# A two-layer hybrid decoder on eight cores: another QKV chain, element-wise work offered to more engines, second norms in a fixed order, and weight loads moved in their queue

## The chip, the cores and the metric

One Trainium2 chip, eight cores, the same program on each with other data: core c takes prompt sequence c and four of the 32 decode rows. The metric is the device time of the slowest core in microseconds. Some runs fall into a slower state, in which one die's cores show a lower granted clock (in one run of the first batch below, four cores took 1698 to 1702 us at 0.81 and the other four 1444 to 1450 at 0.99).

## The reference, cut to what matters

```python
# per layer, for prompt rows (causal) and decode rows (with caches)
h = rmsnorm(x, norm1_g);  proj = h @ w_in               # u | q k v | gb gc gh
y_pool = pool_mix(u)                                    # windows 2/4/8/16
q = partial_rope(rmsnorm(q, q_norm_g), pos)             # per head of 64; rotary on the first 16 dims
k = partial_rope(rmsnorm(k, k_norm_g), pos)             # k and v also go out as the new caches
y_attn = three dilated windows of 2 heads, merged by their softmax denominators
y_conv = gb * conv3(gc * gh)
x = x + concat(y_pool, y_attn, y_conv) @ w_out
x = x + square(relu(rmsnorm(x, norm2_g) @ w_up)) @ w_down
# two layers; 2048 prompt rows + 32 decode rows per core = 5 blocks of 416 columns
```

## The kernel before

The kernel plans its own instruction streams when it is built. Each piece of work is a small process with a priority. It asks for operations with an estimated cost, waits for events and takes buffers from pools. A list scheduler steps through estimated time and appends each operation to one engine's program. `anyof` offers an operation to several engines, and the one that can take it first in the plan gets it. **The plan is static: on the chip every engine runs its list in order, and a PE instruction that waits holds up all behind it.** Weights are loaded by DMAs that the Pool engine issues, in the order of Pool's list.

```python
def dp(n, fn, r, w):                       # DVE or Pool
    return anyof(dve2(n, fn, r, w), pool(n, fn, r, w))

def sumsq(l, which, b, X, s, s, src):      # sum of squares of block b (second norm, and layer 1's first)
    yield acq(PNORM)
    ...
    yield ops(act(BL, ... AF.Square ...))                       # chunk 0 into acc
    for c in range(1, 8):
        ...
        yield ops(act(BL, ... AF.Square ...))                   # ACT
        K.spawn(freeing(dp(BL, ... acc = acc + t ...)))         # DVE or Pool
    bi = yield late(1, lambda bi: pe([... matmul(ones, acc) ...]))

def qkv(l, blk, g, pr):                    # one tile: 256 rows, q k v of two heads; PQKV = Pool([0] * 2) in flight
    ...
    pb0 = yield late(J, ... 16 matmuls into two PSUM banks ...)
    yield ops(act(256 * J, ... Square of q,k from PSUM into sqv ...))
    ...                                    # v * row scale, from PSUM on DVE
    yield ops(dve(256 * J, ... tensor_reduce sqv -> ss ...))
    yield ops(act ... Ln ..., act ... Ln ...);  yield ops(act ... Exp ...)          # rs
    yield ops(dve(256 * J, ... q4 = PSUM q,k * rs ...))         # only now can the two banks go
    yield wait(ev("vq", l, blk, g, pr));  K.release(BANKS, ...);  K.release(PQKV, 0)
    ...                                    # rotary on q4, DVE or Pool
    yield ops(anyof(pool(... cast q4 -> qb bf16 ...), dvec(...), act(...)))
    ...                                    # transposes of qb on PE

def up(l, fb, b, fc):
    ...                                    # 8 matmuls, then PSUM * norm scale on DVE
    yield ops(act(BL, ... Relu ...))
    yield ops(act(BL, ... Square -> bf16 ...))

# weights of the first MLP quarter (fb == 0)
wu, wd = proj_done, qk_done + [ev("xres", l, b, 7) for b in (0, 1)]
```

The MLP goes over four quarters of d_ff. A w_up or w_down quarter comes in four pieces of 512 KB (as bf16), and each down-matmul group reads all four pieces of its w_down quarter.

Of the kernel before, what the change touches and what calls it, by code (L numbers as in the profile page):

```python
# [25 lines left out]
BL = NTOK // NB  # L26
# [523 lines left out]
def build_program():  # L550
# [234 lines left out]
    SQ = [m([128, 512], F32, ("sq", i)) for i in range(2)]  # L785
    m = Mem(XO + SV * XB, XO + SV * XB + XB)
# [66 lines left out]

    def pe(items):

        cost, rw = 0.0, []
        for n, _, r, w in items:
            rw.append((cost, r, w))
            cost += max(n / 2400.0 + 0.0025, 0.056)
        return ("pe", cost, lambda: [S.op("pe", fn, r, w) for _, fn, r, w in items], rw)  # L860
# [21 lines left out]
    PQKV = Pool([0] * 2)  # L882
# [95 lines left out]
    def sumsq(l, which, b, X, s, si, src):  # L978
# [24 lines left out]
        else:  # L1003
            ai = yield acq(PSQR)
            acc, ka = sqr(ai), ("sqr", ai)
            yield ops(act(BL, lambda e: e.activation(out=acc, in_=X[:, si, 0, :], func=AF.Square), [("x", s, 0)], [ka]))
            for c in range(1, 8):
# [4 lines left out]
                yield ops(act(BL, lambda e: e.activation(out=out, in_=X[:, si, c, :], func=AF.Square), [("x", s, c)], [k]))  # L1012
# [91 lines left out]
    def norm2(l, b):  # L1104
        s = SLOTR[b]
        bi = yield from sumsq(l, 1, b, X, s, s, [ev("xm", l, b, c) for c in range(8)])
        yield wait(*[ev("om", l, x, oc) for x in ((0, 1), (2, 3), (4,), (4,), ())[b] for oc in range(8)], *r_free(l, b))
# [198 lines left out]
    def qkv(l, blk, g, pr):  # L1306
# [52 lines left out]
        yield ops(act(256 * J, lambda e: e.activation(out=sqv, in_=pq[0:R, :, 0:256], func=AF.Square), kp, [ksq]))  # L1359
        rt = RT[0:R, 0, tt:tt + J].unsqueeze(2)  # L1360
        if need:
# [3 lines left out]
            K.spawn(seq([], later(dve(128 * J, lambda e: e.tensor_tensor(out=qv, in0=pq[0:R, :, 256:384], in1=rv_, op=ALU.mult), kp + kt, [kq]), ev("vq", l, blk, g, pr)),  # L1365
                        later(act(128 * J, lambda e: e.copy(out=vd, in_=qs), [kq], kv), ev("vc", l, blk, g, pr))), 1000 * l + 100 + 30 * (blk or 0) + 2 * g + pr + 0.5)
# [4 lines left out]
        o = [dve(256 * J, lambda e: e.tensor_reduce(out=ss[0:R, 0:4 * J], in_=sqv.rearrange("p j (a c) -> p (j a) c", a=4), axis=AX.X, op=ALU.add), [ksq], [kss])]  # L1371
        yield ops(*o)
# [3 lines left out]
        q4 = qf[0:R, 0:J, 0:256].rearrange("p j (a c) -> p j a c", a=4)  # L1376
        rb = rs[0:R, 0:4 * J].rearrange("p (j a) -> p j a", j=J).unsqueeze(3).to_broadcast([R, J, 4, 64])
        yield ops(dve(256 * J, lambda e: e.tensor_tensor(out=q4, in0=pq[0:R, :, 0:256].rearrange("p j (a c) -> p j a c", a=4), in1=rb, op=ALU.mult), kp + [krs], [kq]))  # L1378
        K.release(PS4, s4)
        yield wait(ev("vq", l, blk, g, pr))  # L1380
        for j in range(J):
            K.release(BANKS, pb0 + j)
        K.release(PQKV, 0)
        if g > 0 and not smp:
            K.spawn(vshuffle(l, blk, g, pr, vi), 1000 * l + 100 + 50 * blk)
        ri = yield acq(PROT)
        kr = ("rot", ri)
        t0 = 16 if smp else 4 * blk + tis[0]
        rot = [ROTB[ri][0:R, k, 0:4 * J, :].rearrange("p (j a) c -> p j a c", j=J) for k in range(2)]
        xr = q4[:, :, :, 0:16]  # L1390
        tb = [ROPE[0:R, k, t0:t0 + J, :].unsqueeze(2).to_broadcast([R, J, 4, 16]) for k in range(2)]
        g16 = GQK[0:R, 0:64].rearrange("p (a c) -> p a c", a=4).unsqueeze(1).to_broadcast([R, J, 4, 16])
        yield ops(dp(64 * J, lambda e: e.tensor_tensor(out=xr, in0=xr, in1=g16, op=ALU.mult), [kq, "gqk"], [kq]))  # L1393
        yield ops(*[dp(65 * J, lambda e, k=k: e.tensor_tensor(out=rot[k], in0=xr, in1=tb[k], op=ALU.mult), [kq, "rope"], [kr]) for k in range(2)])  # L1394
        yield ops(*[dp(32 * J, lambda e, h=h, op=op: e.tensor_tensor(out=xr[:, :, :, 8 * h:8 * h + 8], in0=rot[0][:, :, :, 8 * h:8 * h + 8], in1=rot[1][:, :, :, 8 - 8 * h:16 - 8 * h], op=op), [kr], [kq]) for h, op in ((0, ALU.subtract), (1, ALU.add))])
        K.release(PROT, ri)
# [7 lines left out]
        def store():  # L1404
            o = []
            for jj, j in enumerate(tis):
                if smp:
                    for n in range(4):
                        o.append(ld(lambda e, n=n: e.dma_start(out=o_kv_s[g][l, n, WINS[g] - 8:WINS[g], :], in_=qf[8 * n:8 * n + 8, 0, 128:384]), 8192, 1024, r=[kq], slot=("kvo", fi)))
                    continue  # L1410
# [3 lines left out]
                o.append(ld(lambda e, jj=jj, dst=dst: e.dma_start(out=dst, in_=qf[:, jj, 128:384]), 131072, 1024, r=[kq], slot=("kvo", fi)))  # L1414
# [6 lines left out]
        if turn:  # L1421
# [4 lines left out]
        qi, qo = qf[0:R, 0:J, 0:256], qb[0:R, 0:J, :]  # L1426
        yield ops(anyof(pool(256 * J, lambda e: e.tensor_copy(out=qo, in_=qi), [kq], [kb], False), dvec(256 * J, lambda e: e.tensor_copy(out=qo, in_=qi), [kq], [kb]),
                        act(256 * J, lambda e: e.copy(out=qo, in_=qi), [kq], [kb])))
        if need:
# [447 lines left out]
    K.run()  # L1877
    assert K.live == 0

    S.emit(es)  # L1880
    es.close()
    return nc

# [77 lines left out]
```

## Time and profile before

| | before |
|---|---|
| time, median of the first 4 runs (range) | 1462.38 us (1460.24 to 1463.35) |
| spans of the cores in the profile | 1452.6 to 1461.6 us |
| mean granted PE clock | 0.981 to 0.988 |
| PE busy | 1393.2 us, 95% |

In the trace a matmul of the MLP lasts 0.34 us while the next one starts 0.18 us after it, and a matmul at half clock counts as busy all the same, so busy time hides small losses. The lines that concern us carry these numbers in the kernel before: L1702 up-projection, L1724 down-projection, L1333 QKV, L1153 the other projections, L1679 out-projection, L1016 the ones-matmul of a norm's sum, L1716 squared relu, L1378 the q,k product that frees the banks.

### The profile page before, as it was taken

How to read it: one execution, taken by the hardware profiler on the slowest of the kernel's cores; microseconds unless marked ns; L12 is line 12 of the kernel's file. 1: busy time of each engine (PE TensorE's matmuls, PEld its weight loads, DVE VectorE, ACT ScalarE, POOL GpSimd, SP SyncE). 2: the span in 40 equal slices, each digit the busy share in tenths (PEclk: the TensorE clock that was granted, in tenths of full speed). 3: DMA queues.
4: the chain of work that ended last, by engine and by line, in shares of the span. 5: the costliest groups of instructions: out<-in, count | busy, mean ns of one | idle time of the engine just before them, and what ended most of it. 6: DMA issues, size and time to landing. Idle time of an engine off the chain costs nothing.

```text
span 1461.6 us, 28003 instructions; the slowest of 8 cores (1452.6 to 1461.6 us)
## 1 busy us (share of the span) xinstructions
PE 1393.2 (95%) x8921; PEld 793.2 (54%) x8921; DVE 800.9 (55%) x1503; ACT 727.4 (50%) x1536; POOL 323.3 (22%) x495
## 2 busy tenths in 40 slices
PE   6999989899999999999999899996999999999998
PEld 3555656455555555555555565553555555555554
DVE  2878767664444444446577877865344444444443
ACT  4656557674244243347756556567243433523532
POOL 4557546410000000000025654640001001000000
PEclk9999989999999999999999999998899999999999
DMA  9750573880690573152245152489019319200122
GB/s 209 188 81 27 89 141 117 209 117 1 97 170 2 87 104 76 31 93 94 61 91 121 28 99 64 151 169 155 3 34 157 77 17 160 63 28 1 48 94 94
DMA packets 81677, 133.31 MB, mean 91 GB/s; under 512 B 14008, under 2 KB 70520, under 8 KB 81152
## 3 DMA queue, kind: packets, MB, share of 16 engines
q0 software_dynamic: 53952, 79.29, 30.6%
q1 hardware_dynamic: 18880, 49.10, 12.8%
q10 hardware_dynamic: 8704, 3.15, 0.9%
q8 instruction: 75, 1.23, 0.3%
q14 instruction: 66, 0.54, 0.1%
HBM read 159.63 MB, written 47.90 MB: 142 GB/s over the span
## 4 chain that ended last, share of the span: by engine, by line
PE 84%; DMA 5%; issue 3%; DVE 3%; ACT 2%; POOL 2%; DVEq 0%; SPq 0%; ACTq 0%; POOLq 0%
PE psum L1724 31%; PE psum L1702 29%; PE psum L1153 8%; PE psum L1333 7%; PE psum L1679 5%; DMA big<-w_down 3%; DMA big<-xin 2%; PE psum L1548 1%; POOL big L851 1%; PE psum L1439 1%; PE psum L991 0%; DMA big<-xpark 0%; DVE big L1371 0%; PE psum L1523 0%; DVE big L1378 0%
## 5 line engine op out<-in xcount | busy, mean ns | idle before, releaser
L1724 PE MATMUL psum<-big 128*128 128x416 bf16 x2560 | 460.2, 341 | 14.7 <-DMA big<-w_down 10.7
L1702 PE MATMUL psum<-big 128*128 128x416 bf16 x2560 | 457.2, 339 | 2.9 <-DMA big<-w_up 1.3
L1715 ACT ACTIVATE big<-big 128x416 f32<-128x416 f32 x320 | 175.0, 548 | 414.1 <-DVE big L1713 413.2
L1724 PEld LDWEIGHTS psum<-big 128*128 128x128 bf16 x2560 | 250.1, 98 | 217.9 <-issue 21.2
L1702 PEld LDWEIGHTS psum<-big 128*128 128x128 bf16 x2560 | 249.1, 98 | 203.4 <-issue 5.7
L1727 DVE TENSOR_TENSOR big<-psum,big 128x416 f32<-128x416 f32 x320 | 189.1, 591 | 248.0 <-PE psum L1724 248.0
L1713 DVE TENSOR_TENSOR big<-psum,big 128x416 f32<-128x416 f32 x320 | 189.0, 591 | 243.9 <-PE psum L1702 181.8
L1716 ACT ACTIVATE big<-big 128x416 bf16<-128x416 f32 x320 | 174.8, 548 | 41.7 <-PE psum L1702 1.3
L1153 PE MATMUL psum<-big 128*128 128x416 bf16 x880 | 172.0, 346 | 8.7 <-DVE big L1654 2.2
L1333 PE MATMUL psum<-big 128*128 128x384 bf16 (+1 forms) x816 | 144.0, 331 | 4.7 <-ACT big L1535 1.8
L1153 PEld LDWEIGHTS psum<-big 128*128 128x128 bf16 x880 | 84.0, 100 | 76.9 <-issue 18.3
L852 ACT ACTIVATE big<-big 128x416 bf16<-128x416 f32 (+3 forms) x135 | 85.2, 636 | 72.7 <-DVE big L1683 26.8
L1333 PEld LDWEIGHTS psum<-big 128*128 128x128 bf16 (+1 forms) x816 | 78.3, 99 | 58.5 <-issue 10.9
L963 POOL DMA_DIRECT2D big<-w_up x32 | 24.0, 768 | 385.8 <-PE psum L1702 368.2
L1679 PE MATMUL psum<-big 128*128 128x416 bf16 x480 | 88.3, 343 | 1.7 <-DVE big L1378 0.8
L851 POOL TENSOR_SCALAR big<-big 128x416 bf16<-128x416 f32 (+4 forms) x46 | 64.1, 1394 | 51.2 <-DVE big L1683 23.5
L1679 PEld LDWEIGHTS psum<-big 128*128 128x128 bf16 x480 | 46.6, 99 | 40.2 <-issue 4.9
L1683 DVE TENSOR_TENSOR big<-psum,big 128x416 f32<-128x416 f32 x80 | 46.4, 587 | 23.3 <-PE psum L1679 19.5
L1359 ACT ACTIVATE big<-psum 128x512 f32<-128x512 f32 (+1 forms) x54 | 30.7, 569 | 53.8 <-PE psum L1333 52.8
L1394 POOL TENSOR_TENSOR big<-big 128x128 f32<-128x128 f32 (+1 forms) x79 | 41.3, 523 | 61.1 <-DVE big L1393 51.6
L1371 DVE TENSOR_REDUCE big<-big 128x8 f32<-128x512 f32 (+1 forms) x54 | 35.2, 651 | 18.0 <-ACT big L1359 16.1
L1374 ACT ACTIVATE big<-big 128x4 f32<-128x4 f32 (+1 forms) x102 | 30.3, 297 | 27.1 <-DVE big L1371 22.7
(133 smaller groups left out, 1089.7 us busy)
## 6 DMA issues: line engine op xcount, KB each, us to landing
big<-w_up POOLq DMA_DIRECT2D x32, 512.0 KB, 19.0
big<-w_down POOLq DMA_DIRECT2D x32, 512.0 KB, 15.6
kv_s<-c SPq DMA_DIRECT2D x8, 2040.0 KB, 16.9
big<-xin_r POOLq DMA_DIRECT2D x10, 832.0 KB, 13.5
xpark<-big SPq DMA_DIRECT2D x10, 832.0 KB, 4.2
big<-xpark POOLq DMA_DIRECT2D x10, 832.0 KB, 8.8
yout<-big SPq DMA_DIRECT2D x20, 416.0 KB, 2.5
big<-xin POOLq DMA_DIRECT2D x8, 832.0 KB, 13.1
```

The source lines that it names most:

```text
L851: f = lambda e: e.tensor_scalar(out=out, in0=in_, scalar1=g, scalar2=None, op0=ALU.mult)
L852: return anyof(act(n, lambda e: e.activation(out=out, in_=in_, func=AF.Copy, scale=g), r, w, True), dvec(n, f, r, w), pool(n, f, r, w, False))
L1153: bi = yield late(1, lambda bi: pe([(BL, lambda e, d=d: e.matmul(bank(bi)[:, 0:BL], lhsT=wa(l, nm, i, d), rhs=HT[:, d, BL * b:BL * b + BL] ...
L1333: pb0 = yield late(J, lambda pb0: pe([(384, lambda e, d=d, j=j, jj=jj: e.matmul(bank(pb0 + jj)[0:R, 0:384].rearrange("p (k n) -> p k n", k ...
L1679: bi = yield late(1, lambda bi: pe([(BL, lambda e, c=c: e.matmul(bank(bi)[:, 0:BL], lhsT=WO[c // 2][:, c % 2, 128 * oc:128 * oc + 128], rh ...
L1683: yield ops(dve(BL, lambda e: e.tensor_tensor(out=X[:, s, oc, :], in0=bank(bi)[:, 0:BL], in1=X[:, s, oc, :], op=ALU.add), [("ps", bi), ("x ...
L1702: bi = yield late(1, lambda bi: pe([(BL, lambda e, d=d: e.matmul(bank(bi)[:, 0:BL], lhsT=WU[i][:, d, 128 * fc:128 * fc + 128], rhs=HT[:, d ...
L1713: yield ops(dve(BL, lambda e: e.tensor_tensor(out=rl, in0=bank(bi)[:, 0:BL], in1=VB[b], op=ALU.mult), [("ps", bi), kvb(b)], [kr]))
L1715: yield ops(act(BL, lambda e: e.activation(out=rl, in_=rl, func=AF.Relu), [kr], [kr]))
L1716: yield ops(act(BL, lambda e: e.activation(out=AT[a][:, fc, :], in_=rl, func=AF.Square), [kr], [("at", a, fc)]))
L1724: bi = yield late(1, lambda bi: pe([(BL, lambda e, f=f: e.matmul(bank(bi)[:, 0:BL], lhsT=WD[i][:, f, 128 * oc:128 * oc + 128], rhs=AT[a][: ...
L1727: yield ops(dve(BL, lambda e: e.tensor_tensor(out=X[:, s, oc, :], in0=bank(bi)[:, 0:BL], in1=X[:, s, oc, :], op=ALU.add), [("ps", bi), ("x ...
```

## The change

Its intent: free the QKV banks early, run rotary beside the norm instead of after it, take load off ACT, finish norms in the order in which the MLP wants them, and have each first w_down quarter land right behind its w_up quarter.

```diff
+    def squared(n, out, x, r, w):
+        f = lambda e: e.tensor_tensor(out=out, in0=x, in1=x, op=ALU.mult)
+        return anyof(act(n, ... AF.Square ...), dve2(n, f, r, w), pool(n, f, r, w))
-    PQKV = Pool([0] * 2)
+    PQKV = Pool([0] * 3)
 # sumsq
-            yield ops(act(BL, ... AF.Square ...))
+            yield ops(squared(BL, ...))                          # both places
 # norm2(l, b)
+        i = ORDER[l][0].index(b)
+        if i:
+            yield wait(ev("n2", l, ORDER[l][0][i - 1]))
         bi = yield from sumsq(l, 1, b, X, s, s, ...)
+        K.fire(ev("n2", l, b))
 # qkv
+        K.spawn(... anyof(dve(256 * J, qf = PSUM q,k), act(...)) ...)      # copy out at once
+        def free_banks():
+            yield wait(ev("vq", ...), ev("qe", ...), ev("sqd", ...))       # v, copy, square done
+            ... K.release(BANKS, ...); K.release(PQKV, 0) ...
+        def rope():
+            yield wait(ev("qe", ...))                                      # on the unscaled copy
+            ... rotary as before ...
         yield ops(act(... Square ...)); reduce; Ln; Exp
-        yield ops(dve(256 * J, ... q4 = PSUM * rs ...))
+        yield wait(ev("rope", ...))
-        yield ops(anyof(... cast q4 -> qb ...))
+        # tile whose k is stored: k *= rs; qb.q = q * rs; qb.k = copy of k.  Other tiles:
+            yield ops(dp(256 * J, ... qb = q4 * rs ...))
 # up
-        yield ops(act(BL, ... Relu ...))
+        f = lambda e: e.tensor_scalar(out=rl, in0=rl, scalar1=0.0, scalar2=None, op0=ALU.max)
+        yield ops(anyof(act(... Relu ...), dvec(BL, f, ...), pool(BL, f, ..., False)))
 # weights, fb == 0
-                wu, wd = proj_done, qk_done + [ev("xres", l, b, 7) for b in (0, 1)]
+                wu, wd = proj_done, qk_done
 # after planning: these DMA issues move right behind another one in Pool's list
+    shift([("wd", 0, h) for h in range(4)], 0, (("wu", 0, 3), 0))          # layer 0
+    shift([("wd", 0, h) for h in range(4)], 2, (("wu", 0, 3), 2))          # layer 1
+    shift([("wo", i) for i in range(3)], 1, (("cvt", 0), 5))               # layer 1's w_out
```

More of the change, by code (lines that the diff above doesn't have):

```diff
@@ L785, in build_program @@
     SQ = [m([128, 512], F32, ("sq", i)) for i in range(2)]
+    for i in range(3):
+        r = S.regions["qf", i]
+        rv_ = S.region(("qfv", i), r.lo, r.hi)
+        r.overl.remove(rv_)
+        rv_.overl.remove(r)
     m = Mem(XO + SV * XB, XO + SV * XB + XB)
@@ L852, in scaled @@
         return anyof(act(n, lambda e: e.activation(out=out, in_=in_, func=AF.Copy, scale=g), r, w, True), dvec(n, f, r, w), pool(n, f, r, w, False))
+    def squared(n, out, x, r, w):
+        f = lambda e: e.tensor_tensor(out=out, in0=x, in1=x, op=ALU.mult)
+        return anyof(act(n, lambda e: e.activation(out=out, in_=x, func=AF.Square), r, w), dve2(n, f, r, w), pool(n, f, r, w))
     def pe(items):
@@ L1005, in sumsq @@
             acc, ka = sqr(ai), ("sqr", ai)
-            yield ops(act(BL, lambda e: e.activation(out=acc, in_=X[:, si, 0, :], func=AF.Square), [("x", s, 0)], [ka]))
+            yield ops(squared(BL, acc, X[:, si, 0, :], [("x", s, 0)], [ka]))
             for c in range(1, 8):
@@ L1011, in sumsq @@
                 out, t, k = (sqr(i), sqr(i).bitcast(F32), ("sqr", i)) if c % 2 else (SS[i], SS[i], ("ss", i))
-                yield ops(act(BL, lambda e: e.activation(out=out, in_=X[:, si, c, :], func=AF.Square), [("x", s, c)], [k]))
+                yield ops(squared(BL, out, X[:, si, c, :], [("x", s, c)], [k]))
                 K.spawn(freeing(dp(BL, lambda e, t=t: e.tensor_tensor(out=acc, in0=acc.bitcast(F32), in1=t, op=ALU.add), [ka, k], [ka]),
@@ L1358, in qkv @@
             vd = vv.rearrange("p j (h c) -> p j h c", h=3)[:, :, 0:3:2, :]
-        yield ops(act(256 * J, lambda e: e.activation(out=sqv, in_=pq[0:R, :, 0:256], func=AF.Square), kp, [ksq]))
+        prio = 1000 * l + 100 + 30 * (blk or 0) + 2 * g + pr
+        qk_in, qk_out = pq[0:R, :, 0:256], qf[0:R, 0:J, 0:256]
+        K.spawn(seq([], later(anyof(dve(256 * J, lambda e: e.tensor_copy(out=qk_out, in_=qk_in), kp, [kq]), act(256 * J, lambda e: e.copy(out=qk_out, in_=qk_in), kp, [kq])), ev("qe", l, blk, g, pr))), prio)
         rt = RT[0:R, 0, tt:tt + J].unsqueeze(2)
+        kqv = ("qfv", fi)
         if need:
@@ L1364, in qkv @@
             qs = qv if smp else qv.rearrange("p j (h c) -> p j h c", h=2)
-            K.spawn(seq([], later(dve(128 * J, lambda e: e.tensor_tensor(out=qv, in0=pq[0:R, :, 256:384], in1=rv_, op=ALU.mult), kp + kt, [kq]), ev("vq", l, blk, g, pr)),
-                        later(act(128 * J, lambda e: e.copy(out=vd, in_=qs), [kq], kv), ev("vc", l, blk, g, pr))), 1000 * l + 100 + 30 * (blk or 0) + 2 * g + pr + 0.5)
+            K.spawn(seq([], later(dve(128 * J, lambda e: e.tensor_tensor(out=qv, in0=pq[0:R, :, 256:384], in1=rv_, op=ALU.mult), kp + kt, [kqv]), ev("vq", l, blk, g, pr)),
+                        later(act(128 * J, lambda e: e.copy(out=vd, in_=qs), [kqv], kv), ev("vc", l, blk, g, pr))), 1000 * l + 100 + 30 * (blk or 0) + 2 * g + pr + 0.5)
         else:
@@ L1370, in qkv @@
             K.fire(ev("vc", l, blk, g, pr))
-        o = [dve(256 * J, lambda e: e.tensor_reduce(out=ss[0:R, 0:4 * J], in_=sqv.rearrange("p j (a c) -> p (j a) c", a=4), axis=AX.X, op=ALU.add), [ksq], [kss])]
-        yield ops(*o)
+        def free_banks():
+            yield wait(ev("vq", l, blk, g, pr), ev("qe", l, blk, g, pr), ev("sqd", l, blk, g, pr))
+            for j in range(J):
+                K.release(BANKS, pb0 + j)
+            K.release(PQKV, 0)
+            if g > 0 and not smp:
+                K.spawn(vshuffle(l, blk, g, pr, vi), 1000 * l + 100 + 50 * blk)
+        K.spawn(free_banks(), prio)
+        q4 = qf[0:R, 0:J, 0:256].rearrange("p j (a c) -> p j a c", a=4)
+        rb = rs[0:R, 0:4 * J].rearrange("p (j a) -> p j a", j=J).unsqueeze(3).to_broadcast([R, J, 4, 64])
+        xr = q4[:, :, :, 0:16]
+        def rope():
+            yield wait(ev("qe", l, blk, g, pr))
+            ri = yield acq(PROT)
+            kr = ("rot", ri)
+            rot = [ROTB[ri][0:R, k, 0:4 * J, :].rearrange("p (j a) c -> p j a c", j=J) for k in range(2)]
+            tb = [ROPE[0:R, k, tt:tt + J, :].unsqueeze(2).to_broadcast([R, J, 4, 16]) for k in range(2)]
+            g16 = GQK[0:R, 0:64].rearrange("p (a c) -> p a c", a=4).unsqueeze(1).to_broadcast([R, J, 4, 16])
+            yield ops(dp(64 * J, lambda e: e.tensor_tensor(out=xr, in0=xr, in1=g16, op=ALU.mult), [kq, "gqk"], [kq]))
+            yield ops(*[dp(65 * J, lambda e, k=k: e.tensor_tensor(out=rot[k], in0=xr, in1=tb[k], op=ALU.mult), [kq, "rope"], [kr]) for k in range(2)])
+            yield ops(*[dp(32 * J, lambda e, h=h, op=op: e.tensor_tensor(out=xr[:, :, :, 8 * h:8 * h + 8], in0=rot[0][:, :, :, 8 * h:8 * h + 8], in1=rot[1][:, :, :, 8 - 8 * h:16 - 8 * h], op=op), [kr], [kq]) for h, op in ((0, ALU.subtract), (1, ALU.add))])
+            K.release(PROT, ri)
+            K.fire(ev("rope", l, blk, g, pr))
+        K.spawn(rope(), prio)
+        yield ops(act(256 * J, lambda e: e.activation(out=sqv, in_=qk_in, func=AF.Square), kp, [ksq]))
+        K.fire(ev("sqd", l, blk, g, pr))
+        yield ops(dve(256 * J, lambda e: e.tensor_reduce(out=ss[0:R, 0:4 * J], in_=sqv.rearrange("p j (a c) -> p (j a) c", a=4), axis=AX.X, op=ALU.add), [ksq], [kss]))
         K.release(PSQ, si)
@@ L1375, in qkv @@
         yield ops(act(8, lambda e: e.activation(out=rs[0:R, 0:4 * J], in_=rs[0:R, 0:4 * J], func=AF.Exp, scale=-0.5), [krs], [krs]))
-        q4 = qf[0:R, 0:J, 0:256].rearrange("p j (a c) -> p j a c", a=4)
-        rb = rs[0:R, 0:4 * J].rearrange("p (j a) -> p j a", j=J).unsqueeze(3).to_broadcast([R, J, 4, 64])
-        yield ops(dve(256 * J, lambda e: e.tensor_tensor(out=q4, in0=pq[0:R, :, 0:256].rearrange("p j (a c) -> p j a c", a=4), in1=rb, op=ALU.mult), kp + [krs], [kq]))
-        K.release(PS4, s4)
-        yield wait(ev("vq", l, blk, g, pr))
-        for j in range(J):
-            K.release(BANKS, pb0 + j)
-        K.release(PQKV, 0)
-        if g > 0 and not smp:
-            K.spawn(vshuffle(l, blk, g, pr, vi), 1000 * l + 100 + 50 * blk)
-        ri = yield acq(PROT)
-        kr = ("rot", ri)
-        t0 = 16 if smp else 4 * blk + tis[0]
-        rot = [ROTB[ri][0:R, k, 0:4 * J, :].rearrange("p (j a) c -> p j a c", j=J) for k in range(2)]
-        xr = q4[:, :, :, 0:16]
-        tb = [ROPE[0:R, k, t0:t0 + J, :].unsqueeze(2).to_broadcast([R, J, 4, 16]) for k in range(2)]
-        g16 = GQK[0:R, 0:64].rearrange("p (a c) -> p a c", a=4).unsqueeze(1).to_broadcast([R, J, 4, 16])
-        yield ops(dp(64 * J, lambda e: e.tensor_tensor(out=xr, in0=xr, in1=g16, op=ALU.mult), [kq, "gqk"], [kq]))
-        yield ops(*[dp(65 * J, lambda e, k=k: e.tensor_tensor(out=rot[k], in0=xr, in1=tb[k], op=ALU.mult), [kq, "rope"], [kr]) for k in range(2)])
-        yield ops(*[dp(32 * J, lambda e, h=h, op=op: e.tensor_tensor(out=xr[:, :, :, 8 * h:8 * h + 8], in0=rot[0][:, :, :, 8 * h:8 * h + 8], in1=rot[1][:, :, :, 8 - 8 * h:16 - 8 * h], op=op), [kr], [kq]) for h, op in ((0, ALU.subtract), (1, ALU.add))])
-        K.release(PROT, ri)
+        yield wait(ev("rope", l, blk, g, pr))
         left = [1]
@@ L1408, in store @@
                     for n in range(4):
-                        o.append(ld(lambda e, n=n: e.dma_start(out=o_kv_s[g][l, n, WINS[g] - 8:WINS[g], :], in_=qf[8 * n:8 * n + 8, 0, 128:384]), 8192, 1024, r=[kq], slot=("kvo", fi)))
+                        o.append(ld(lambda e, n=n: e.dma_start(out=o_kv_s[g][l, n, WINS[g] - 8:WINS[g], :], in_=qf[8 * n:8 * n + 8, 0, 128:384]), 8192, 1024, r=[kq, kqv], slot=("kvo", fi)))
                     continue
@@ L1413, in store @@
                 dst = o_kv_p[0][l] if g == 0 else o_kv_p[1][l, j] if g == 1 else o_kv_p[2][l, blk, j]
-                o.append(ld(lambda e, jj=jj, dst=dst: e.dma_start(out=dst, in_=qf[:, jj, 128:384]), 131072, 1024, r=[kq], slot=("kvo", fi)))
+                o.append(ld(lambda e, jj=jj, dst=dst: e.dma_start(out=dst, in_=qf[:, jj, 128:384]), 131072, 1024, r=[kq, kqv], slot=("kvo", fi)))
             yield ops(*o)
@@ L1425, in qkv @@
         qb, kb = QB[bi], ("qb", bi)
-        qi, qo = qf[0:R, 0:J, 0:256], qb[0:R, 0:J, :]
-        yield ops(anyof(pool(256 * J, lambda e: e.tensor_copy(out=qo, in_=qi), [kq], [kb], False), dvec(256 * J, lambda e: e.tensor_copy(out=qo, in_=qi), [kq], [kb]),
-                        act(256 * J, lambda e: e.copy(out=qo, in_=qi), [kq], [kb])))
+        qo = qb[0:R, 0:J, :].rearrange("p j (a c) -> p j a c", a=4)
         if need:
+            q2, k2, rq, rk = q4[:, :, 0:2], q4[:, :, 2:4], rb[:, :, 0:2], rb[:, :, 2:4]
+            yield ops(dp(128 * J, lambda e: e.tensor_tensor(out=k2, in0=k2, in1=rk, op=ALU.mult), [kq, krs], [kq]))
+            yield ops(dp(128 * J, lambda e: e.tensor_tensor(out=qo[:, :, 0:2], in0=q2, in1=rq, op=ALU.mult), [kq, krs], [kb]),
+                      anyof(pool(128 * J, lambda e: e.tensor_copy(out=qo[:, :, 2:4], in_=k2), [kq], [kb], False), dvec(128 * J, lambda e: e.tensor_copy(out=qo[:, :, 2:4], in_=k2), [kq], [kb]),
+                            act(128 * J, lambda e: e.copy(out=qo[:, :, 2:4], in_=k2), [kq], [kb])))
+            K.release(PS4, s4)
             k48 = q4[:, :, 2:4, 16:64]
@@ L1432, in qkv @@
             K.fire(ev("kg", l, blk, g, pr))
+        else:
+            yield ops(dp(256 * J, lambda e: e.tensor_tensor(out=qo, in0=q4, in1=rb, op=ALU.mult), [kq, krs], [kb]))
+            K.release(PS4, s4)
         used()
@@ L1714, in up @@
         K.release(BANKS, bi)
-        yield ops(act(BL, lambda e: e.activation(out=rl, in_=rl, func=AF.Relu), [kr], [kr]))
+        f = lambda e: e.tensor_scalar(out=rl, in0=rl, scalar1=0.0, scalar2=None, op0=ALU.max)
+        yield ops(anyof(act(BL, lambda e: e.activation(out=rl, in_=rl, func=AF.Relu), [kr], [kr]), dvec(BL, f, [kr], [kr]), pool(BL, f, [kr], [kr], False)))
         yield ops(act(BL, lambda e: e.activation(out=AT[a][:, fc, :], in_=rl, func=AF.Square), [kr], [("at", a, fc)]))
@@ L1878, in build_program, with shift @@
     assert K.live == 0
+    def shift(slots, nth, past):
+        q = S.ops["pool"]
+        hit = lambda s, n: [o for o in q if o.dma_slot == s][n]
+        moved = [hit(s, nth) for s in slots]
+        for o in moved:
+            nxt = q[q.index(o) + 1]
+            while nxt in moved:
+                nxt = q[q.index(nxt) + 1]
+            nxt.waits = nxt.waits + o.waits
+            nxt.wait_vals.update(o.wait_vals)
+            q.remove(o)
+        i = q.index(hit(*past)) + 1
+        q[i:i] = moved
+    shift([("wd", 0, h) for h in range(4)], 0, (("wu", 0, 3), 0))
+    shift([("wd", 0, h) for h in range(4)], 2, (("wu", 0, 3), 2))
+    shift([("wo", i) for i in range(3)], 1, (("cvt", 0), 5))
     S.emit(es)
```

## The prediction

> **What bounds the kernel now.** I read the spans of the cores first: 1452.6 to 1461.6 us, both dies near clock 0.98, so there is one state to explain. Next came the table by stage (slowest core; columns: stretch in us, its length, then busy us and instruction count of PE, PEld, DVE, ACT, POOL, then PE clock, DMA share, GB/s):
>
> ```profile
> 0.00:60.00 60.00, 42.73 (x177) 22.70 (x178) 29.62 (x66) 31.70 (x71) 32.57 (x58) 0.94 0.91 202
> 120.00:235.00 115.00, 107.51 (x1031) 67.22 (x1028) 84.12 (x183) 67.97 (x175) 62.10 (x106) 0.96 0.52 106
> 300.00:510.00 210.00, 209.09 (x1189) 115.85 (x1188) 93.79 (x162) 90.44 (x171) 8.90 (x12) 1.00 0.47 76
> 735.00:940.00 205.00, 194.94 (x1671) 119.19 (x1670) 162.38 (x338) 118.95 (x301) 104.55 (x166) 0.99 0.38 85
> 940.00:1030.00 90.00, 74.35 (x406) 39.96 (x404) 54.68 (x101) 59.60 (x116) 27.64 (x37) 0.91 0.82 153
> 1030.00:1240.00 210.00, 210.00 (x1192) 116.36 (x1190) 87.56 (x149) 77.03 (x141) 11.89 (x16) 1.00 0.43 75
> ```
>
> The MLP stretches (300 to 735, 1030 to 1455) are pure PE at full clock: the chain of waits there is matmul after matmul, 11.25 us for 64. Nothing on another engine shortens them. What can be gained lies in the mixers (0 to 300, 735 to 940) and where layer 1's MLP starts (940 to 1030, PE busy 74 of 90 us at clock 0.91). The waits of the PE name the places (all of the run; us in total, times, longest):
>
> ```profile
> PE psum L991 <- ACT big L990: 12.3, 2, 6.9
> PE psum L1724 <- DMA big<-w_down: 10.7, 1, 10.7
> PE psum L1573 <- DVE big L1571: 4.6, 2, 4.3
> ...
> PE psum L1439 <- DVE big L1427: 1.9, 1, 1.9
> PE psum L1333 <- ACT big L1535: 1.8, 1, 1.8
> PE psum L1153 <- DVE big L1378: 1.8, 2, 1.5
> PE psum L1523 <- DVE big L1378: 1.7, 1, 1.7
> PE psum L1724 <- issue: 1.6, 1, 1.6
> PE psum L1724 <- ACT big L1716: 1.6, 1, 1.6
> ```
>
> L991 is the first norm of layer 0, which the change leaves alone. The second line is one wait for down-projection weights. The waits on L1378 (q and k times their norm, the read that frees the PSUM banks) and L1427 (their cast ahead of the transposes) belong to the QKV chain. Last I read finer tables around the two worst places, in the same columns:
>
> ```profile
> 208.00:220.00 12.00, 9.22 (x83) 6.10 (x82) 6.00 (x14) 6.67 (x14) 4.19 (x6) 0.57 1.10 245
> 256.00:268.00 12.00, 7.39 (x91) 4.89 (x90) 6.34 (x11) 7.17 (x14) 5.35 (x6) 0.72 0.62 179
> 985.00:1015.00 30.00, 25.29 (x139) 13.27 (x137) 17.42 (x33) 26.18 (x56) 4.45 (x6) 0.99 1.10 158
> 1015.00:1032.00 17.00, 6.32 (x20) 2.93 (x21) 5.13 (x9) 4.82 (x10) 0.00 (x0) 0.51 0.46 76
> ```
>
> The reader is to see that a wait costs twice: first the idle time, then matmuls at about half clock (0.57, 0.72, 0.51). In 985 to 1015 the DMA engines are full and ACT, 26 of 30 us busy, is the fullest engine after PE.
>
> **What the Trainium skill says.** "TensorE: Matmul & The Clock Gate", section "What's actually happening": after an idle window of about 3.4 us the PE clock falls to half, and returns after a busy window of that length. The trace agrees: a 10.7 us wait is followed by a stretch at 0.51. "PSUM — Partial Sum Buffer", section "PSUM bank collisions raise a hardware error": two engines must not touch one bank at once, reads included. So the new PSUM copy and the square take turns; the kernel's own scheduler already orders readers of a bank on different engines, and in the trace they don't overlap. "DMA: Bandwidth & Descriptors", section "Issuing engines are not separate DMA queues": all transfers share 16 engines. The trace shows the Pool queue's transfers landing in order of issue while these are full, so order in that queue is order of arrival.
>
> **The change part by part.**
>
> (a) *Weights.* Layer 1's down-projection needs four pieces of w_down. In the Pool timeline three are issued at 972.6, then three w_up pieces of the next quarter; the fourth w_up then waits 8.3 us for the PE, and the last w_down piece comes at 988.3, behind seven transfers that aren't needed for another 100 us. It lands 37 us later, and the PE idles from 1015.0 to 1025.7. Afterwards the clock records say half speed until 1031.6: 5.9 us at half lose 3.0. The change puts all four pieces right behind the first four w_up, which land at 987.7. Pieces land 3 to 5 us apart there, so the fourth should land near 988 + 4 x 4 = 1004. It is wanted no sooner than 985 + 128 up-matmuls x 0.176 = 1008. The wait goes: 10.7 + 3.0 = 13.7; I count 13.
>
> (b) *Relu and squares on any of three engines.* In 985 to 1015 ACT runs 15 relus (8.0 us) and 19 squares of the second norm (10.2 us) on top of 15 squared outputs. PE waits there, w_down aside: w_up 1.3, DVE 0.9, ACT 0.8 and 1.6, in all 4.6. The ACT ones should go, w_up stays: 2.5. In the later MLP it is worth nothing, since PE has no waits there. The norms in fixed order only make sure that block 0 is ready first.
>
> (c) *QKV chain.* Now: square (ACT 0.60), reduce (DVE 0.68), two logs (0.30 each), exp (0.20), product from PSUM (DVE 0.69), then rotary, cast (DVE 0.44, Pool 0.69, ACT 0.62). Banks are held from the square to the product. For the tile at 200.94 in the timeline the product ends at 206.95, 6.0 us; the mean over 54 tiles is 4.4. After: q and k are copied out at once (like the product: 0.69 on DVE, or like the square: 0.60 on ACT), rotary runs on the unscaled values beside the norm, and the scaling writes bf16, so the cast goes. Held: square 0.60, copy 0.69, v product 0.41 in turns, with hops an estimate of 2.0 to 2.5 us. Work per tile: copy in (0.6 to 0.7), cast out (0.44 to 0.69), the scaling moved to SBUF, where Pool may do it (estimate 1.3 us, from 1.06 for 416 elements). Net about +0.1 us x 54 tiles = 5 us over three engines, hidden: DVE is 79% busy in 735 to 940 and no bound yet. Where keys are stored, three half-size operations take the place of two full ones (0.41 + 0.41 + 0.3 against 0.69 + 0.44): even.
> On the path: 196 to 220 has waits of 1.1, 1.7, 1.9 and 0.8 (5.5), and its half clock (209.0 to 219.2, some 8 us of it in matmuls) loses 4; elsewhere L1378 holds the PE 1.5 and 0.8. Sum 11.8. Other waits will move in (banks for three tiles at a time, the chain still 4 us deep), so I count 60%: 7.
>
> (d) *End of attention in layer 0.* L1573 waits 4.3 us for a mask product, because its exponential stands on ACT behind norm squares; half clock then loses 2.3 more. Squares on other engines, and QKV finishing earlier so that projections are left as filler, could remove it: 40% of 6.6, so 3.
>
> (e) *Layer 1's mixer* waits mostly on attention and decode rows (L1535, L1632, L1654): 1. Moving layer 1's w_out behind the second cache load: about 0, w_out now lands 140 us before use.
>
> (f) *New waits*, above all for w_up in layer 0: -1.5.
>
> Sum: 13 + 2.5 + 7 + 3 + 1 - 1.5 = 25. 1462.4 - 25 = 1437.
>
> **The rivals.** *Only the weights count.* PE is 95% busy by the page, the mixers are a static schedule in which each shift of a tile opens a new gap; then (a) alone remains: 1449. For it: the waits of (c) are many and short. Against: they cluster in one place that lost its clock. *The gaps close nearly everywhere*: (a) 13.7, (b) 4.6, (c) 11.8, (d) 6.6, some 37 us: 1425. For it: DVE and Pool have room in every stage. Against: the plan is made with estimated costs; Pool's one-input product takes 1.39 us for 416 elements here, far more than the 0.63 that the kernel's planner assumes, so work offered to Pool can come late. *DMA becomes the bound in layer 0.* In before, layer 0's first w_up lands by 217, early. The wd move makes sense only if w_up now comes after the last QKV; then residual reloads, w_up and w_down queue together ahead of 280, as in layer 1, and a wait of 5 to 10 us at layer 0's first up-matmuls eats part of the gain: 1444. *Slower* would need DVE at its limit in the mixers: 5 us more on 162 of 205 doesn't do that.
>
> **Range and chances.** (a) is nearly sure, 12 to 14; the rest is 11 give or take 9. Predicted 1437, range 1424 to 1451. Faster by over 2% needs less than 1433.1, that is 29 us saved: 0.34. Within 2%: 0.64. Slower: 0.02.
>
> **What would show it.** Right: no PE wait on w_down; the stretch after layer 1's first up-projections at clock 1.00; the fourth w_down landing some 15 us after the fourth w_up; no clock drop near 210; copies within 2.5 us of the square; ACT below 20 of 30 us at layer 1's MLP start; MLP stretches unchanged, 210 us for 1190 matmuls. Wrong: a new wait on w_up or the reloads near 280, PE waits on the new copy or on Pool products, or the half clock merely moved elsewhere.

## The result, and the profile after

| | before | after |
|---|---|---|
| time, median (range) | 1461.45 us (13 runs, fast ones 1459.95 to 1463.35) | 1432.62 us (8 runs, 1431.69 to 1433.71; the record lists a ninth fast one, 1436.18, that its summary leaves out) |
| ratio of the fast runs | | 0.9804 (0.9794 to 0.9813) |
| mean granted clock of the cores | 0.981 to 0.988 | 0.993 to 0.997 |
| half-clock time between 40 and 1420 us, slowest core | 44.4 us | 3.4 us |

A ratio is the mean time of one kernel's fast runs over that of the other's fast runs of the same rounds, so not quite the ratio of the medians quoted. 29 us went, 2% to within the interval, so which side of 2% it lies on stays undecided. Half-clock time counts by the clock records and includes time in which the PE stands still; only the part in which matmuls run costs more.

The table by stage of the changed kernel, slowest core, in the columns used in the prediction and shifted to the same work where that starts earlier:

```profile
0.00:60.00 60.00, 42.27 (x184) 22.85 (x185) 29.67 (x66) 31.62 (x71) 32.93 (x58) 0.94 0.92 202
120.00:235.00 115.00, 109.02 (x1053) 68.89 (x1052) 96.06 (x193) 73.83 (x184) 66.44 (x113) 1.00 0.30 65
290.00:500.00 210.00, 210.00 (x1194) 116.32 (x1193) 102.53 (x180) 91.48 (x173) 28.75 (x28) 1.00 0.49 83
724.00:926.00 202.00, 194.23 (x1681) 119.16 (x1679) 165.68 (x342) 124.02 (x316) 108.31 (x179) 1.00 0.36 82
926.00:1000.00 74.00, 72.73 (x413) 40.26 (x412) 53.78 (x99) 47.90 (x88) 31.75 (x42) 1.00 1.02 200
1000.00:1210.00 210.00, 209.74 (x1193) 116.20 (x1191) 95.35 (x165) 80.44 (x150) 21.70 (x23) 1.00 0.46 78
...
972.00:998.00 26.00, 24.87 (x142) 13.77 (x142) 19.49 (x37) 20.08 (x42) 10.45 (x11) 1.00 1.10 158
998.00:1015.00 17.00, 17.00 (x98) 9.48 (x97) 13.21 (x24) 9.25 (x20) 4.01 (x4) 1.00 0.35 58
```

The MLP stretches are what they were: 210 us for some 1190 matmuls. Layer 1's MLP start (last two rows) runs 98 matmuls in 17 us at clock 1.00, where the kernel before ran 20 in 17 us at 0.51. The DMA engines are as full as before (1.10). The longest waits of the PE in the changed kernel, in the same columns as before:

```profile
PE psum L1000 <- ACT big L999: 12.1, 2, 6.4
PE psum L1009 <- ACT sqr L1008: 3.9, 6, 1.2
PE psum L1346 <- ACT big L1565: 3.4, 5, 0.9
PE psum L1469 <- ACT big L1565: 2.5, 3, 1.4
PE psum L1709 <- DVE big L1713: 2.2, 2, 1.4
PE psum L1603 <- DVE big L1601: 2.1, 1, 2.1
```

The line numbers have moved: L1000 is the first norm (the old L991, untouched), L1346 QKV, L1565 the softmax exponential, L1603 the old L1573. No wait on w_down is left. Apart from the first norm, no single wait is longer than 2.1 us.

To see where the time went, I counted matmuls in the traces and compared when the same piece of work starts, core by core, and took the median of the eight differences to the kernel before:

| start of | after minus before |
|---|---|
| layer 0, first down-matmul | -8.5 us |
| layer 1, last out-projection matmul | -13.9 us |
| layer 1, first down-matmul | -14.9 us |
| layer 1, 64th down-matmul | -30.0 us |
| last down-matmul | -29.0 us |

So layer 0 up to its MLP gave 8.5, layer 1's mixer 5.4 more, and the start of layer 1's MLP 16.

From the same traces, the two PSUM banks of a QKV tile are held, from the first to the last read, 4.4 us on average before and 2.5 after (54 tiles on the slowest core).

### The profile page after: what moved, and what is told of

It reads as the page before. It is cut to its first block, busy times and chain, and to the rows that moved or that the text cites. A ratio compares the mean times of both kernels' runs of the same rounds, so it can differ in the third digit from the quotient of the medians.

```text
span 1431.1 us, 28187 instructions; the slowest of 8 cores (1426.5 to 1431.1 us)
## 1 busy us (share of the span) xinstructions
PE 1381.2 (97%) x8921; PEld 787.9 (55%) x8921; DVE 824.9 (58%) x1544; ACT 709.9 (50%) x1494; POOL 371.2 (26%) x552
## 4 chain that ended last, share of the span: by engine, by line
PE 87%; DMA 3%; issue 3%; POOL 2%; DVE 2%; ACT 2%; SPq 0%; ACTq 0%; DVEq 0%; POOLq 0%
PE psum L1755 31%; PE psum L1732 31%; PE psum L1166 8%; PE psum L1346 7%; PE psum L1709 6%; DMA big<-xin 1%; PE psum L1578 1%; POOL big L856 1%; DMA big<-ckt 1%; PE psum L1469 1%; ACT big L1565 1%; DMA big<-xin_r 0%; POOL big L1745 0%; PE psum L1000 0%; PE psum L1603 0%
## 5 line engine op out<-in xcount | busy, mean ns | idle before, releaser
L1732 PE MATMUL psum<-big 128*128 128x416 bf16 x2560 | 457.1, 339 | 1.8 <-ACT big L1121 1.1
L1732 PEld LDWEIGHTS psum<-big 128*128 128x128 bf16 x2560 | 249.1, 98 | 202.3 <-issue 6.2
L1746 ACT ACTIVATE big<-big 128x416 f32<-128x416 f32 x284 | 156.0, 550 | 396.3 <-DVE big L1743 394.9
L1346 PE MATMUL psum<-big 128*128 128x384 bf16 (+1 forms) x816 | 142.3, 329 | 5.3 <-ACT big L1565 3.4
L857 ACT ACTIVATE big<-big 128x416 bf16<-128x416 f32 (+3 forms) x146 | 92.8, 640 | 86.2 <-DVE big L1713 34.3
L1346 PEld LDWEIGHTS psum<-big 128*128 128x128 bf16 (+1 forms) x816 | 78.2, 98 | 59.1 <-issue 10.6
L856 POOL TENSOR_SCALAR big<-big 128x416 bf16<-128x416 f32 (+6 forms) x37 | 50.1, 1355 | 61.3 <-DMA big<-xin 17.0
L1745 POOL TENSOR_SCALAR big<-big 128x416 f32<-128x416 f32 x25 | 34.9, 1399 | 53.3 <-DVE big L1743 52.7
L1408 POOL TENSOR_TENSOR big<-big 128x128 f32<-128x128 f32 (+1 forms) x71 | 36.5, 515 | 37.5 <-DVE big L1407 22.9
L1302 DVE SCALAR_TENSOR_TENSOR big<-big 128x416 f32<-128x416 f32 (+1 forms) x60 | 41.0, 687 | 3.9 <-POOL big L856 2.5
```

The costliest lines, as they stand in the source:

```text
L856: f = lambda e: e.tensor_scalar(out=out, in0=in_, scalar1=g, scalar2=None, op0=ALU.mult)
L857: return anyof(act(n, lambda e: e.activation(out=out, in_=in_, func=AF.Copy, scale=g), r, w, True), dvec(n, f, r, w), pool(n, f, r, w, False))
L1346: pb0 = yield late(J, lambda pb0: pe([(384, lambda e, d=d, j=j, jj=jj: e.matmul(bank(pb0 + jj)[0:R, 0:384].rearrange("p (k n) -> p k n", k ...
L1732: bi = yield late(1, lambda bi: pe([(BL, lambda e, d=d: e.matmul(bank(bi)[:, 0:BL], lhsT=WU[i][:, d, 128 * fc:128 * fc + 128], rhs=HT[:, d ...
L1746: yield ops(anyof(act(BL, lambda e: e.activation(out=rl, in_=rl, func=AF.Relu), [kr], [kr]), dvec(BL, f, [kr], [kr]), pool(BL, f, [kr], [k ...
```

## The experiments

All kernels gave right results. Each batch ran on one chip beside its own runs of the kernel before. The medians of before were 1461.85 (first batch), 1463.80 (second) and 1463.72 (third). Differences of some 2 us between batches are not read.

### First batch: the late piece of weights, and what a reshuffle is worth

*The kernel before with one DMA issue moved* (`shift` as in the change):

```diff
+    shift([("wd", 0, 3)], 2, (("wd", 0, 2), 2))      # layer 1's 4th w_down piece, ahead of 7 others
```

> The kernel before, with one thing moved: the last of the four w_down pieces that layer 1's MLP reads first goes right behind the other three in the Pool queue, ahead of seven transfers that are needed later. Weights theory (the wait of 10.7 us and the half clock behind it are the one cost): 13 to 16 us saved, 1446 to 1449 us, no PE wait on w_down, clock 1.00 after the first up-projections of layer 1, and everything before 985 us as it was. Rival (ACT, 26 of 30 us busy there, takes the wait over): PE waits on relu or squared relu grow from 2.5 us to 6 or more and less than 9 us are saved.

Measured: 1453.98 us, ratio 0.9948 (0.9924 to 0.9971): 8 us, not 14. The piece landed at 1001, in time, and the wait for it is gone. The waits of the PE from 985 to 1030 us in that run:

```profile
PE psum L1724 <- ACT big L1716: 3.6, 2, 2.0
PE psum L1702 <- DVE big L1713: 0.9, 1, 0.9
PE psum L1724 <- ACT big L1108: 0.8, 1, 0.8
```

L1724 now waits 2.0 us for the squared relu on ACT at the place where it waited for the weights, and the clock fell to half for 6.8 us from 1013.8, 5.5 of them after that wait. The rival had a share: in the kernel before, the wait for the weights stood in front of one for ACT. While PE waited for the DMA, ACT caught up unseen.

Nor was the half clock the price of the weights alone. This is the PE in the kernel before (start, time, engine, line, form; in brackets the idle time ahead and its cause):

```profile
1011.87 1.04 PE L1724 MATMUL psum<-big 128*128 128x416 bf16 x5 [0.85 <-ACT big L1108]
1014.50 0.50 PE L1724 MATMUL psum<-big 128*128 128x416 bf16 x1 [1.59 <-ACT big L1716]
1025.68 3.63 PE L1724 MATMUL psum<-big 128*128 128x416 bf16 x10 [10.69 <-DMA big<-w_down]
```

Its clock records say half speed from 1014.5, half a us before the long wait begins, behind the two short waits for ACT. Both short waits are still there with the piece moved, and the clock falls there on all eight cores without any wait for the weights. So the move took away 10.7 us, brought 2.0, and left the half clock much as it was (after the wait 5.5 us against 5.9 on the two slowest cores, 3.1 against 3.8 in the median of eight). By this estimate it saves some 9 us, near the 8 measured.

*The changed kernel with that piece put back late*:

```diff
     shift([("wo", i) for i in range(3)], 1, (("cvt", 0), 5))
+    shift([("wd", 0, 3)], 2, (("wd", 1, 2), 2))
```

> The changed kernel, with that last w_down piece of layer 1 moved back behind the next quarter's transfers, where the kernel before had it; all else stays. Weights theory: it lands some 25 us later than in the changed kernel (near 1005 instead of 981), PE waits near 996 for about 10 us and then runs 5 us or so at half clock: 10 to 14 us lost, 1443 to 1447 us. Rival (the earlier mixer end gives the transfers enough time, so the order no longer matters): under 3 us lost.

Measured: 1444.83 us, ratio 0.9886 against 0.9804 for the changed kernel: 12 us lost, as expected of the weights, though the wait was shorter than the 10 us expected.

```profile
PE psum L1755 <- DMA big<-w_down: 6.8, 1, 6.8
```

Half clock runs from 1001.7 to 1008.6, 4.1 us of it after the wait; the changed kernel has neither, so here both are the weights' own. By estimate they cost 6.8 + 4.1/2, some 9 us, and that is what the median core lost at its 64th down-matmul (9.1). The slowest core lost 12, since the wait differs between cores (5.9 to 7.9 us). As a mean over all cores of the fast runs the late piece costs 9.4 us here (against runs of the changed kernel in other rounds) and 7.5 in the kernel before. That it costs more where no other wait stands behind it fits, but the gap is smaller than the 12 and 8 of the slowest cores suggest.

*Both kernels with one constant of the planner changed*:

```diff
-SLACK = 0.8
+SLACK = 0.85
```

> The kernel before, with one constant of its planner changed (the margin that a matmul leaves after its producer, 0.80 to 0.85 us). It is meant as a measure of what a mere reshuffle of the static plan does. The plan that comes out happens to have the last w_down piece of layer 1 right behind the other three. Weights theory: that alone gives 13 to 16 us, so 1444 to 1452 us with some 3 us either way for the reshuffle. Rival (the plan is so tuned that any reshuffle costs several us elsewhere): 1455 us or more in spite of the piece.

> The changed kernel with the same constant changed (0.80 to 0.85 us). The order of the weights' transfers stays as it is. If a reshuffle is worth little, 1430 to 1436 us; if the changed kernel's plan was picked among many, it loses 3 to 8 us: 1436 to 1441. Either way the difference says how large an effect of one part must be to count as that part's own.

Measured: the kernel before went to 1451.73 us, ratio 0.9930 (0.9905 to 0.9955); the changed one to 1434.77, ratio 0.9818. A constant that means nothing for the hardware took 10 us off the kernel before, because in the new plan the w_down piece was no longer behind seven others. Its 64th down-matmul of layer 1 came 11.3 us earlier, and nothing of the mixers gained over 1.2 us. **The late piece was an accident of the plan.** The changed kernel lost some 2 us, with overlapping intervals, so differences of that size between variants below mean nothing by themselves. This is one reshuffle of each kernel and no measure of how far others would go.

### Second batch: relief of ACT, and the QKV chain alone

*The kernel before, relu offered to three engines; and the same with the piece on time:*

```diff
-        yield ops(act(BL, ... Relu ...))
+        yield ops(anyof(act(... Relu ...), dvec(BL, f, ...), pool(BL, f, ..., False)))
```

> The kernel before, with only the relu of the up-projections offered to ACT, DVE or Pool; the last w_down piece stays late. The run with the piece moved saved 8 us and not 14, and showed two new PE waits on the squared relu on ACT (3.6 us and then 6.8 us of half clock). Hiding theory (in the kernel before, the wait for the weights hides a wait for ACT, each alone is worth little): under 2 us saved, 1459 to 1463 us, the wait for w_down longer than 10.7 us because the PE comes to it sooner. Rival (relief of ACT is worth its 2.5 us by itself): 1457 to 1460 us.

> Both together: the kernel before with relu on any of three engines and the last w_down piece of layer 1 on time. Hiding theory: the two parts are worth more together than the sum of each alone (8 and about 0): 12 to 16 us saved, 1446 to 1450 us, no wait of over 1 us on the squared relu and clock 1.00 after it. Rival (the parts add up): 8 to 10 us, 1452 to 1454 us.

Measured: 1464.97 us (ratio 1.0008, 0.9983 to 1.0033) and 1459.63 us (0.9973, 0.9948 to 0.9998). The time of the first fits the hiding theory, but its sign did not come: the wait for w_down was not longer than 10.7 us but 1.4 on the slowest core (1.0 to 5.1 over the cores), because PE now stood elsewhere first. The second refutes the theory as I had put it: the two parts together gave less than the piece alone (the 64th down-matmul of layer 1 came 4.6 us earlier, against 9.9 with the piece alone). A PE wait of the run with both, which the run with relu alone has at the same length:

```profile
PE psum L1016 <- DVE sqr L1013: 6.0, 1, 6.0
```

L1016 is the ones-matmul of a later block's norm. The planner, thinking its running sum nearly done, had put it into PE's list ahead of the first down-matmuls. On the chip the sum, with its squares on ACT and its adds on DVE between the work of the up-projections, was 6 us late, and the whole list stood. So I took the trouble to be not the sum of ACT's work, but norms of later blocks mixed into work that is needed now; the third batch tests that.

*The changed kernel with relu and squares on ACT alone again:*

```diff
-        return anyof(act(n, ... AF.Square ...), dve2(n, f, r, w), pool(n, f, r, w))
+        return act(n, ... AF.Square ...)
-        yield ops(anyof(act(... Relu ...), dvec(BL, f, ...), pool(BL, f, ..., False)))
+        yield ops(act(... Relu ...))
```

> The changed kernel, with relu and the squares of the norms on ACT alone again; the weights on time and the new QKV chain stay. Hiding theory: with the weights on time ACT is what is waited for at layer 1's MLP start, so 4 to 8 us come back there (waits on relu or squared relu, perhaps a half clock window): 1436 to 1442 us. Rival (the norms in fixed order are enough): within 2 us of the changed kernel, 1432 to 1435 us.

Measured: 1431.70 us, ratio 0.9779 (0.9754 to 0.9804), no slower than the changed kernel (0.9804) and, with touching intervals from different rounds, not shown to be faster. Offering this work to three engines is worth nothing measurable in the changed kernel.

*The kernel before with the new QKV chain and three tiles in flight alone* (the hunks of `qkv` and `PQKV` above):

> The kernel before with the new QKV chain and three tiles in flight alone; relu and squares on ACT, no issue moved by hand. The plan that comes out has layer 1's w_down in the right order by itself, so at layer 1's MLP start it is like the run with the piece moved. QKV theory: layer 0's first down-projection comes 5 to 9 us earlier than in the kernel before, layer 1's last out-projection a further 2 to 5 us, and 8 to 9 us come from the weights: 1440 to 1447 us. Rival (the mixers' gain is not the chain's but that of the squares moved off ACT): layer 0 gains less than 3 us: 1450 us or more.

Measured: 1449.08 us, ratio 0.9900 (0.9875 to 0.9925): slower than expected, for a reason neither theory had. Layer 0's last out-projection came 9.6 us earlier, so the chain does work, yet its first down-matmul came 4.9 us *later* than in the kernel before (the 7.6 of a later expectation compares the two slowest cores):

```profile
PE psum L1021 <- DVE sqr L1018: 7.4, 1, 7.4
```

A norm's ones-matmul again (L1021 here), now in layer 0, from 288.8 to 296.2 us, with half clock from 292.4 to 302.6. In layer 1's mixer the chain gained another 7 us by the same milestones (+4.7 at layer 0's last down-matmul, -2.5 at layer 1's last out-projection).

### Third batch: the order of the norms, the two parts together, the depth

*The kernel before with the second norms in fixed order alone* (the `norm2` hunk, and nothing else):

> The kernel before with the second norms in a fixed order alone (five lines: block b waits until the norm of the block ahead of it has its sum). Seen so far: relief of ACT in the kernel before gave nothing, and PE stood 6 to 7 us at a norm's ones-matmul whose running sum was late. The plan that comes out also has the last w_down piece on time by itself. Order theory (what cost time at layer 1's MLP start, apart from the piece, was the norms of all blocks mixed on ACT and DVE): no PE wait of over 1.5 us after 985 us, layer 1's 64th down-matmul 14 to 18 us earlier, 1443 to 1448 us with the mixers as before. Rival (only the piece counts): 8 us as in the run with the piece moved, 1453 us, with the waits on the squared relu.

Measured: 1445.84 us, ratio 0.9881 (0.9865 to 0.9896), 17.5 us from four lines. The plan puts w_down right by itself, as the expectation said. The rows from 985 us on, and then all waits of the PE there:

```profile
985.00:1009.00 24.00, 22.68 (x129) 12.37 (x129) 15.82 (x29) 20.38 (x43) 3.72 (x5) 1.00 1.09 155
1009.00:1026.00 17.00, 17.00 (x98) 9.43 (x97) 12.25 (x23) 13.64 (x29) 0.68 (x1) 1.00 0.39 64
```

```profile
PE psum L1706 <- DVE big L1717: 1.3, 1, 1.3
```

ACT is 20.4 of 24 us busy, as full as in the kernel before, and PE hardly waits. Against the run with the piece alone (8 us), the order brings 9 more; in the traces the median core has 7 more at layer 1's 64th down-matmul, 1.6 of them already at layer 1's last out-projection.

*The changed kernel without the fixed order:*

> The changed kernel without the fixed order of the second norms, all else kept, squares and relu on three engines too. Order theory: PE waits again at norm sums or squared relus at the start of one MLP or both, with half clock behind them: 5 to 12 us lost, 1438 to 1445 us. Rival (spreading over three engines or the moved weights do it): within 2 us of the changed kernel, 1431 to 1435 us.

Measured: 1442.26 us, ratio 0.9858: 10 us lost, all before layer 0's down-projections (its first down-matmul 2.2 us later than in the kernel before instead of 8.5 earlier).

```profile
284.76 0.50 PE L1025 MATMUL psum<-sqr,onesr 128*128 128x416 f32 x1
292.51 0.69 PE L1025 MATMUL psum<-sqr,onesr 128*128 128x416 f32 x1 [7.25 <-DVE sqr L1022]
```

In this timeline of PE the sum of one block's norm goes through, and the next stands 7.25 us ahead of the up-projections. With the order, in the changed kernel, up-projections (L1732) lie between these two matmuls:

```profile
283.99 0.50 PE L1025 MATMUL psum<-sqr,onesr 128*128 128x416 f32 x1
285.15 8.62 PE L1732 MATMUL psum<-big 128*128 128x416 bf16 x48 [0.66 <-DVE big L1713]
293.45 0.50 PE L1025 MATMUL psum<-sqr,onesr 128*128 128x416 f32 x1
```

*The kernel before with the QKV chain, three tiles and the fixed order:*

> The kernel before with the new QKV chain, three tiles in flight and the fixed order of the norms; relu and squares on ACT, no issue moved, w_down gated as before. If these two parts are the whole change: layer 0's first down-projection 6 to 9 us earlier (the chain alone had it 7.6 us later, with 7.4 us at a norm sum), and 1432 to 1438 us in all. If the issues moved by hand and the three engines still count: 1440 us or more.

Measured: 1444.32 us, ratio 0.9871 (0.9850 to 0.9893), no better than the order alone within the intervals. Layer 0's first down-matmul comes 5.5 us earlier, a little under the 6 to 9 expected, but its 64th comes 5.5 us *later*:

```profile
PE psum L1750 <- DMA big<-w_down: 8.7, 1, 8.7
```

Here the accident of the weights has moved to layer 0. The projections now end after the QKV tiles, so w_up is issued late, only three w_down pieces follow it, and the fourth goes behind the next quarter's w_up. That costs 8.7 us, and half clock runs on for 5.9 us after it. The changed kernel, which moves layer 0's w_down and drops its second gate, has no such wait; no run takes one of these two away alone.

*The changed kernel with two tiles in flight:*

```diff
-    PQKV = Pool([0] * 3)
+    PQKV = Pool([0] * 2)
```

> The changed kernel with two QKV tiles in flight in place of three. If the early release of the PSUM banks is what the new chain gives, a third tile adds little: 1431 to 1436 us. If the depth does it, layer 0's last QKV comes 8 us or more later, and 4 to 8 us are lost: 1437 to 1441 us.

Measured: 1444.66 us, ratio 0.9874: 12 us lost, but not as the depth theory had it. Layer 0's last QKV was as early as with three, and the layer's first down-matmul only 1.4 us later than in the changed kernel. The loss is in layer 1's mixer:

```profile
PE psum L1658 <- DMA big<-ckt: 7.0, 1, 7.0
```

A decode row's key cache is late, and half clock runs on for 6.2 us after the wait. The same matmuls wait 0.7 us for it in the changed kernel, whose w_out transfers stand ahead of that cache load by the third move. With two tiles those w_out transfers land from 846.9 to 856.7 and the cache at 858.7, right behind them. Whether the depth or only this new order of events costs the 12 us is open: no run had two tiles without the third move.

## Why the prediction was right or wrong

The time (1432.6 against 1437) lies in the range. By place the sum came out close: layer 0, (c) + (d) + (f), 8.5 predicted and 8.5 measured; layer 1's MLP start, (a) + (b), 15.5 and 16; layer 1's mixer, (e), 1 and 5.4, which is where the sum of 25 falls short of 29. The causes were less well assigned, so that the match by place is partly luck: in layer 0 the chain alone lost 4.9 us at the first down-matmul, and the 8.5 came only with parts that (c) does not name.

- **(a)** The wait for w_down and its half clock vanished. As a term of the change, 13 was about right: putting the piece back costs 12. As a property of the kernel before it was not, for alone it gave 8: a wait of 2.0 us for ACT stood behind it, and the 3.0 for half clock was for the most part not the weights': the clock fell at 1014.5, before the wait for them began at 1015.0, and it falls there without that wait too. "The trace agrees" says more than the trace shows there. The prediction took the PE's named wait as the whole wait, and as the cause of what followed.
- **(b)** The step that failed: "The norms in fixed order only make sure that block 0 is ready first." That order is worth some 7 to 10 us beside the weights, in the kernel before (in layer 1) and in the changed one (in layer 0). The relief of ACT, to which the 2.5 us went, is worth nothing measurable. I had read "ACT 26 of 30 us busy" as the bound; with the order, ACT was as busy (20.4 of 24) and PE waited once, 1.3 us. The sign of being right, "ACT below 20 of 30 us", did not come in the changed kernel either: from 972 us on it is 23.7 of 30, without loss.
- **(c)** The hold of the banks was estimated at 2.0 to 2.5 us and is 2.5. The clock drop near 210 is gone. That other waits would move in was right, but not which: a norm sum, then w_down in layer 0, each in turn with half clock. The chain's gain (some 10 us at layer 0's last out-projection) reaches the end only with the order and the moved weights.
- **(d)** L1573's wait of 4.3 us fell to 2.1. The order of the norms alone took it to 2.1 in the kernel before as well.
- **(e)** Mis-sized: 1 us predicted, 5.4 measured. The chain alone gave 7 us in that mixer. I had looked only at waits named after the chain's lines and missed that waits named for others can come from banks held by it. That last link is argued, not shown. Moving w_out was counted as nothing; in the run with two tiles its transfers stand ahead of a late cache, so it may hurt there, but no run takes the move away alone, and none shows that it helps.
- **(f)** No wait on w_up in layer 0 came, but the rival's picture was right: w_up and w_down do queue together there, and in the run with chain and order but no hand-made move PE waits 8.7 us, for w_down.

Of the rivals, "only the weights count" is refuted by the 17.5 us of the order, of which the mixers gave only some 2, and by the 13.9 us that the changed kernel gained ahead of layer 1's MLP. "The gaps close nearly everywhere" (1425) came nearest by the number.

Nothing I ran clearly beats the changed kernel. The one with relu and squares on ACT alone ties with it and is simpler.

## What to carry to other kernels

A wait that the profile names can stand in front of another, so take it away alone and see what is left before adding its price to a sum. In a statically ordered kernel, ask of each instruction that waits long whether it had to come first: the order of side work that is needed later (norms of later blocks, weights of later quarters) was worth more here than moving work to idle engines. Where clocks fall, compare the time of the fall with the start of the wait before naming the wait as the cause. And before crediting a part of a change, run a variant that changes the plan for no reason; here that moved one kernel by 10 us and the other by 2.

## What the Trainium skill lacked or had wrong

- "TensorE: Matmul & The Clock Gate", section "What's actually happening", gives an idle window of about 3.4 us for the fall to half clock. In the kernel before a wait of 1.8 us at 838 us, with short matmuls about it, was enough: half clock from 840.5 to 843.9. At 1014.5 the clock fell after 3.4 us in which PE had waited 0.85 and 1.59 us. A wait of 2.1 us at 236 us in the changed kernel, on the other hand, was followed by none. The same page's section "A second HAM failure mode: psum-queue depth-cycling" fits better, but gives no size of idle time.
- "GPSIMD Engine Reference", section 4.1 "Engine selection", says that on GpSimd "1-input is roughly line-rate". Here the one-input relu (a maximum with a constant, 128x416 fp32) took 1.40 us on Pool and 0.38 on DVE, longer than a two-input add of the same size on Pool (1.06 us). A one-input cast of 128x512 took 0.71 us on Pool, so it is not every one-input operation.
- No page that I read says what a late piece in a full queue costs in a chain of semaphores: seven transfers of 512 KB ahead of one piece made 24 us of delay (landing at 1025.4 us in the kernel before, at 1001.4 with the piece moved), at 2.5 to 3.7 us each.
